# Wider logit tiles in the attention of a hybrid decoder layer: two PSUM banks per tile, one mask-and-maximum instruction for up to 1024 keys

## The chip, the cores and the metric

The kernel runs on one core of one Trainium2 chip. The metric is the device time of one execution in microseconds (us). Engines are named as in the profile: PE is TensorE (PEld its weight loads), DVE is VectorE, ACT is ScalarE, POOL is GpSimd, SP is SyncE.

## The reference: what is computed

One decoder layer on x of 2048 rows by 1024 columns, float32: an RMSNorm, one wide projection, a gated short convolution, a sparse attention, gates, an output projection, a SwiGLU feed-forward part and a last RMSNorm. The change touches the attention alone. There an indexer picks 256 keys for each query, and 8 heads of width 64, which share one set of keys and values, attend to the picked keys with a relative-position bias:

```python
logits = jnp.einsum("bthd,btkd->bhtk", q_b, k_sel) * (HEAD_DIM ** -0.5)
logits = logits + bias[...]
logits = jnp.where(valid[:, None], logits, -jnp.inf)
p = jax.nn.softmax(logits, axis=-1)
o = jnp.einsum("bhtk,btkd->bthd", p, v_sel)
```

The kernel gathers nothing. It takes all causal keys, and an additive mask of large negative numbers removes those that were not picked.

## The kernel before, in words

**Stages.** The kernel first makes all projections (with the index scores between them). Then, for each half of the sequence, it runs the attention of that half (`attention(half)`, L562) and the dense part behind it: branch outputs, output projection, feed-forward. In the first dense part ACT also searches the thresholds for the key masks of the second half.

**Attention of a half.** A half has 8 query blocks of 128 rows, taken from the longest to the shortest (`ORDER`): 7 to 0, then 15 to 8. Block b sees n = (b + 1) * 128 keys. A group is one block with 4 of its 8 heads, so a half has 16 groups. The work of a group has two parts:

- `logits` (L621). For each head the n keys are cut into spans of at most 512 (`cuts`, L610). For each span PE makes the logits with two matmuls (`KH` at L639, `KL` at L640) into the PSUM tile `lg`, which is one bank. One fused DVE instruction (L642) then adds the mask, writes the negated logits into the SBUF tile `pr`, and carries the running maximum `mx` from span to span; its scalar start value is the `mx` of the span before. For all spans but the last the mask is `Mt`, straight from memory. For the last it is `MB`, which POOL prepares: the mask copied to float32 (L617, once for each block and each of two tiles) and, over the last 256 keys, mask plus bias (L629, once for each head). When all spans are done, one ACT instruction (L646) makes the exponentials of the whole row in place.
- `values` (L665). In step sb, for each 128 keys, PE transposes the 4 heads' exponentials into a PSUM tile `tpb` (L686). ACT copies it to `ph` (L689), rounded, and DVE subtracts to get the remainder `pl` (L690). Two matmuls, `ph` (L673) and `pl` (L674), add into the PSUM tile `pv`. `spread` (L653) transposes the reciprocal sums through one more `tpb` tile at the first step of a group (L656, copied out by ACT at L658). At the end of a group ACT copies `pv` to `t` (L678) and POOL scales it.

**PSUM.** Eight banks: `LGB` = 3 for `lg`, `7 - LGB` = 4 for `tpb`, 1 for `pv` (L572 to L574).

**Order of the work.** The order of PE in the attention is written by hand: `in_order` (L590) chains every matmul and transpose behind the one before. Within a step PE issues the logits that are due, the transposes of this step, and the products of three steps earlier (`LAG` = 3). `logits_until` (L723) decides which logits are due: those of a group are spread over the steps of the group before it, span by span, and have to be done `LEAD` steps (5 and 4) ahead of their own group. The queues of ACT, DVE, POOL and SP are ordered by a list scheduler, by priority and by its own forecast of what is ready; once written, each queue is served strictly in order.

**SBUF.** The pools of the attention are stacked from the low end, in the order keys and values, `ap` (with `MB`, `ph`, `pl`, `R`, `t`), `few`, and last the ring of `pr` tiles: 12 of 4 KB per partition in the first half, 9 of 8 KB in the second. The pools of the dense part that follows are stacked from both ends; its `raw4` tiles (4 of 4 KB) and its input tiles `x2`/`y4` (8 of 4 KB) come from the high end. A tile may be filled as soon as the older tiles on its bytes are done with, so the first loads of the dense part can start during the attention: its `raw` tiles take `YT` (the convolution's output) and `AT` (the attention's output). ACT rounds them (`y<-raw`, L130) and DVE takes the remainder (L131), for `AT` after adding two halves (L796). The remainders of the first two are queued on DVE behind the eighth remainder `pl` from the end of the attention (`issue_after`, L809).

Of the kernel before, what the change touches and what calls it, by code (L numbers as in the profile page):

```python
# [25 lines left out]
P = 128  # L26
# [26 lines left out]
SOLO = 4  # L53
LEAD = (5, 4)
PHB = 4
LGB = 3
PRB = (12, 9)
EVERY = 6

# [16 lines left out]
def trunk_kernel(tc, x, g_mix, w_in, b_gate, conv_w, w_a, w_b, w_out, rel_bias,  # L76
# [7 lines left out]
    def pool(stack, name, bufs=1, **kw):  # L84
        return stack.enter_context(tc.tile_pool(name=name, bufs=bufs, reuse_waits="tile", **kw))
# [476 lines left out]
    def attention(half):  # L562
# [6 lines left out]
        few = pool(b_stack, f"few{half}")  # L569
        few.tile([P, 32], F32, name="pad")  # L570
        prp = pool(b_stack, f"pr{half}")
        lgp = pool(b_stack, f"lg{half}", bufs=LGB, space=PSUM)  # L572
        tpb = pool(b_stack, f"tpb{half}", bufs=7 - LGB, space=PSUM)
        pvp = pool(b_stack, f"pv{half}", bufs=1, space=PSUM)  # L574
        biasT = kvp.tile([P, NH, 256], F32, name="biasT")
        KH = kvp.tile([P, LH], F32R, name="KH")
# [20 lines left out]
        def setup(b):  # L597
            n = (b + 1) * P
            c, o = divmod(b * P, CH)
            with tc.high_priority(offset=EARLY):  # L600
                q = kvp.tile([P, NH, P], F32R, name="q", tag="q", bufs=2)
                nc.gpsimd.dma_start(out=q, in_=QS[c][:, :, o:o + P].rearrange("h p t -> p h t"))
                if b < 2:
                    Mt = cadd[:, 2 * P - n:]
                else:
                    Mt = kvp.tile([P, LH], BF16, name="Mt", tag="Mt", bufs=2)
                    nc.gpsimd.dma_start(out=Mt[:, 0:n], in_=MS[b])
                if b == ORDER[half][0]:
                    bias_loads()
            cuts = [0] + list(range(CH - P if n % CH == P and n>P else CH, n, CH)) + [n]  # L610
            spans = [(s0, s1 - s0) for s0, s1 in zip(cuts, cuts[1:])]
            lw = spans[-1][1]
            near = min(lw, 2 * P)
            MBs = [ap.tile([P, CH], F32, name="MB", tag="MB", bufs=4) for _ in range(2)]
            if lw > near:
                for MB in MBs:
                    nc.gpsimd.tensor_tensor(MB[:, 0:lw - near], Mt[:, n - lw:n - near],  # L617
                                            zero.broadcast_to([P, lw - near]), op=ALU.add)
            return b, n, q, Mt, spans, near, MBs

        def logits(st, hg, res):  # L621
# [4 lines left out]
            for hh in range(4):  # L626
# [6 lines left out]
                    pr = prp.tile([P, LH], F32, name="pr", tag="pr", bufs=PRB[half])  # L633
                mx = few.tile([P, 5], F32, name="mx", tag="mx", bufs=6)
                for i, (s0, w) in enumerate(spans):
                    lg = lgp.tile([P, CH], F32, name="lg", tag="lg")
                    for o2 in range(0, w, CH):
                        e2 = min(o2 + CH, w)
                        in_order(nc.tensor.matmul(lg[:, o2:e2], q[:, h, :], KH[:, s0 + o2:s0 + e2], start=True, stop=False))  # L639
# [376 lines left out]
```

## Time and profile before

| | |
|---|---|
| median of 3 runs | 3252.79 us (3252.26 to 3253.07) |
| profiled execution, own time | 3258.31 us |
| its span, first to last instruction | 3256.5 us |
[...]
| attention of the first half | about 980 to 1108 us of the span |
| attention of the second half | about 2037 to 2333 us |

The profiled execution is 5.5 us (0.17%) longer than the median of the timed runs. Durations are taken from it, and differences are applied to the median. A PE that is shown as busy need not be at its peak, since the ends of matmuls are modelled; the start of one matmul to the start of the next is the better measure of what it costs.

### The profile page before, as it was taken

The numbers are of one execution on the slowest core, as the hardware profiler recorded it, in microseconds if no ns is written. First come the engines' busy times: TensorE is split into PE (matmuls) and PEld (weight loads), VectorE is DVE, ScalarE is ACT, GpSimd is POOL, SyncE is SP. The second block draws the span as 40 slices with busy tenths as digits, with TensorE's granted clock in tenths as the row PEclk, the third lists the DMA queues.
The fourth block names the chain that finished last, engine by engine and source line by source line (L and its number), as shares of the span: only waits on it lengthen the run. The fifth ranks groups of instructions, "written<-read, shape, count | busy, mean of one in ns | idle before, by whom it ended". The sixth has DMA issues, their size and how long they took to land.

```text
span 3256.5 us, 41205 instructions
## 1 busy us (share of the span) xinstructions
PE 3183.8 (98%) x14723; PEld 2625.9 (81%) x14723; DVE 1655.4 (51%) x3030; ACT 1877.0 (58%) x3630; POOL 777.5 (24%) x684
## 2 busy tenths in 40 slices
PE   8999999999999899999999999999999999999998
PEld 6788888888887678887888888787788888888887
DVE  6344366663528754654535434898853422332234
ACT  6479888779758685677686780787622211111111
POOL 5411122221115422222221222222122222212221
PEclk9999999999999899999999999999999999999999
DMA  7643233332344861222223223222571411111111
GB/s 233 178 141 118 91 99 95 98 99 88 109 126 110 220 230 51 89 75 87 83 62 95 83 62 101 78 57 73 133 245 47 145 50 46 52 51 46 46 46 52
DMA packets 338630, 324.75 MB, mean 100 GB/s; under 512 B 20340, under 2 KB 268360, under 8 KB 338040
## 3 DMA queue, kind: packets, MB, share of 16 engines
q1 hardware_dynamic: 301800, 293.64, 29.3%
q0 software_dynamic: 36624, 28.48, 4.2%
q8 instruction: 115, 1.88, 0.2%
q14 instruction: 91, 0.75, 0.1%
HBM read 248.09 MB, written 75.54 MB: 99 GB/s over the span
## 4 chain that ended last, share of the span: by engine, by line
PE 73%; ACT 12%; DVE 5%; DMA 5%; issue 3%; POOL 1%; SPq 0%; POOLq 0%; DVEq 0%; ACTq 0%
PE mm L156 8%; PE mm L158 8%; PE mm L157 8%; PE gu L156 7%; PE gu L158 7%; PE gu L157 7%; ACT dump L359 6%; PE dn L156 4%; PE dn L158 4%; PE dn L157 4%; PE tpb L686 3%; PE sc L260 2%; PE sc L259 2%; PE pv L673 2%; PE pv L674 2%
## 5 line engine op out<-in xcount | busy, mean ns | idle before, releaser
L359 ACT ACTIVATE dump<-key,nt 128x384 uint8<-128x384 int16 (+27 forms) x420 | 549.0, 1307 | 10.8
L156 PE MATMUL gu<-h2hi,wgu 128*128 128x512 f32 x1408 | 549.0, 390 | 0.0
L157 PE MATMUL gu<-h2lo,wgu 128*128 128x512 f32 x1408 | 548.5, 390 | 0.0
L158 PE MATMUL gu<-h2hi,wgu 128*128 128x512 f32 x1408 | 548.2, 389 | 0.0
L156 PE MATMUL mm<-hThi,whi 128*128 128x512 f32 (+2 forms) x1216 | 472.3, 389 | 0.2 <-ACT hThi L150 0.2
L158 PE MATMUL mm<-hThi,wlo 128*128 128x512 f32 (+2 forms) x1216 | 470.4, 388 | 0.8 <-POOL wlo L131 0.8
L157 PE MATMUL mm<-hTlo,whi 128*128 128x512 f32 (+2 forms) x1216 | 470.4, 387 | 0.0
L971 DVE SCALAR_TENSOR_TENSOR x<-dn,x 128x512 f32<-128x512 f32 x352 | 240.1, 689 | 221.4 <-PE dn L158 221.2
L267 DVE SCALAR_TENSOR_TENSOR acc<-r,iwT,acc 128x512 f32<-128x512 f32 (+2 forms) x266 | 196.1, 737 | 277.8 <-ACT r L262 276.4
L131 POOL TENSOR_TENSOR wlo<-raw,whi 128x512 fp32r<-128x512 f32 (+1 forms) x132 | 176.1, 1336 | 673.0 <-ACT whi L130 600.2
L131 POOL TENSOR_TENSOR hid<-th,hid 128x512 fp32r<-128x512 f32 x88 | 118.0, 1341 | 823.0 <-ACT hid L130 823.0
L157 PEld LDWEIGHTS gu<-h2lo,wgu 128*128 128x128 f32 x1408 | 264.9, 188 | 55.0
L158 PEld LDWEIGHTS gu<-h2hi,wgu 128*128 128x128 f32 x1408 | 264.8, 188 | 55.1
L156 PEld LDWEIGHTS gu<-h2hi,wgu 128*128 128x128 f32 x1408 | 264.9, 188 | 54.9
L156 PE MATMUL dn<-wd,hid 128*128 128x512 f32 x704 | 275.3, 391 | 5.4 <-ACT hid L130 2.9
L158 PE MATMUL dn<-wd,hid 128*128 128x512 f32 x704 | 274.3, 390 | 1.9 <-POOL hid L131 1.9
L131 POOL TENSOR_TENSOR wgu<-raw,wgu 128x1024 fp32r<-128x1024 f32 x88 | 217.4, 2472 | 242.7 <-ACT wgu L130 236.4
L157 PE MATMUL dn<-wd,hid 128*128 128x512 f32 x704 | 274.6, 390 | 0.0
L158 PEld LDWEIGHTS mm<-hThi,wlo 128*128 128x128 f32 (+1 forms) x1216 | 226.7, 187 | 50.3 <-POOL wlo L131 1.1
L954 DVE SCALAR_TENSOR_TENSOR th<-th,gu 128x512 f32<-128x512 f32 x88 | 60.3, 685 | 403.1 <-ACT th L953 365.7
L157 PEld LDWEIGHTS mm<-hTlo,whi 128*128 128x128 f32 (+1 forms) x1216 | 227.0, 187 | 42.6
L156 PEld LDWEIGHTS mm<-hThi,whi 128*128 128x128 f32 (+1 forms) x1216 | 226.9, 187 | 42.6 <-ACT hThi L150 0.6
(201 smaller groups left out, 5806.2 us busy)
## 6 DMA issues: line engine op xcount, KB each, us to landing
raw<-in_w_in_dram SPq DMA_DIRECT2D x124, 256.0 KB
raw<-in_w_ffn_gate_dram SPq DMA_DIRECT2D x44, 512.0 KB
raw<-in_w_ffn_up_dram SPq DMA_DIRECT2D x44, 512.0 KB
raw<-in_w_ffn_down_dram SPq DMA_DIRECT2D x44, 512.0 KB
S<-SD SPq DMA_DIRECT2D x80, 256.0 KB
GT<-f SPq DMA_DIRECT2D x64, 256.0 KB
ta<-GT SPq DMA_DIRECT2D x64, 256.0 KB
S<-SD SPq DMA_DIRECT2D x68, 192.0 KB
```

The costliest lines, as they stand in the source:

```text
L131: lo_eng.tensor_tensor(lo, raw, hi.bitcast(F32), op=ALU.subtract)
L156: nc.tensor.matmul(ps, whi, xhi, start=start, stop=False)
L157: nc.tensor.matmul(ps, whi, xlo, start=False, stop=False)
L158: nc.tensor.matmul(ps, wlo, xhi, start=False, stop=stop)
L259: nc.tensor.matmul(sc[:, 0:w], iqb[:, h, :], IKH[:, s0:s0 + w], start=True, stop=False)
L260: nc.tensor.matmul(sc[:, 0:w], iqb[:, h, :], IKL[:, s0:s0 + w], start=False, stop=True)
L267: nc.vector.scalar_tensor_tensor(acc[:, 0:w], r[:, 0:w], wv, acc[:, 0:w], op0=ALU.mult, op1=ALU.add)
L359: nc.scalar.activation(dump, keys, AF.Sign, bias=nt, accum_out=sm)
L673: in_order(nc.tensor.matmul(pv, V[:, sb, :], ph, start=sb == 0, stop=False))
L674: in_order(nc.tensor.matmul(pv, V[:, sb, :], pl, start=False, stop=sb == b))
L686: in_order(nc.tensor.transpose(tp[:, hh * P:(hh + 1) * P], Ps[hh][:, sb * P:(sb + 1) * P], ident))
L971: nc.vector.scalar_tensor_tensor(x2[tt][:, ns], ps, 0.5, x2[tt][:, ns], op0=ALU.mult, op1=ALU.add)
```

## The change

The logit tile becomes two banks wide and there are two of them; the transposes keep three banks instead of four. A block with up to 1024 keys has one span, a longer block has two, of which the last holds 768 or 1024 keys. `MB` becomes as wide as the last span can be. The inner loop over `o2`, which is in both versions, cuts the matmuls of a span at 512 columns. Nothing else is edited.

```diff
-LGB = 3
+WIDE = 2 * CH
...
-        lgp = pool(b_stack, f"lg{half}", bufs=LGB, space=PSUM)
-        tpb = pool(b_stack, f"tpb{half}", bufs=7 - LGB, space=PSUM)
+        lgp = pool(b_stack, f"lg{half}", bufs=2, space=PSUM)
+        tpb = pool(b_stack, f"tpb{half}", bufs=3, space=PSUM)
...
-            cuts = [0] + list(range(CH - P if n % CH == P and n>P else CH, n, CH)) + [n]
-            spans = [(s0, s1 - s0) for s0, s1 in zip(cuts, cuts[1:])]
+            first = max(0, n - WIDE)
+            if first and n % CH == P:
+                first += 2 * P
+            spans = [(0, n)] if first == 0 else [(0, first), (first, n - first)]
             lw = spans[-1][1]
             near = min(lw, 2 * P)
-            MBs = [ap.tile([P, CH], F32, name="MB", tag="MB", bufs=4) for _ in range(2)]
+            MBs = [ap.tile([P, WIDE], F32, name="MB", tag="MB", bufs=4) for _ in range(2)]
...
-                    lg = lgp.tile([P, CH], F32, name="lg", tag="lg")
+                    lg = lgp.tile([P, WIDE], F32, name="lg", tag="lg")
                     for o2 in range(0, w, CH):
                         e2 = min(o2 + CH, w)
```

## Rows read from the trace of the kernel before

**Rows 1.** The profile page, busy time of PE and its weight loads, and of the other engines: share of the span and number of instructions.

```profile
PE 3183.8 (98%) x14723; PEld 2625.9 (81%) x14723; DVE 1655.4 (51%) x3030; ACT 1877.0 (58%) x3630; POOL 777.5 (24%) x684
```

**Rows 2.** Busy time of each engine by stretch. Columns: stretch and its length in us, then busy us (and instructions) of PE, PEld, DVE, ACT, POOL, then the granted clock, the DMA share and GB/s. The first row is 84 us of the first half's attention, the second the whole attention of the second half, the others 40 us pieces of that.

```profile
978.00:1062.00 84.00, 80.30 (x464) 65.19 (x463) 73.49 (x202) 69.24 (x145) 44.94 (x64) 1.00 0.44 106
2037.00:2336.00 299.00, 285.36 (x1664) 234.61 (x1663) 272.65 (x673) 229.26 (x366) 73.13 (x95) 0.99 0.25 72
...
2080.00:2120.00 40.00, 39.94 (x238) 33.68 (x237) 37.31 (x94) 31.63 (x47) 7.75 (x10) 1.00 0.18 49
2200.00:2240.00 40.00, 37.11 (x215) 30.25 (x214) 35.01 (x84) 29.80 (x50) 10.80 (x14) 1.00 0.36 93
```

**Rows 3.** Timeline of one steady step in the second half, PE and DVE. Columns: start us, duration us, engine, line, operation, tiles, size, count merged into the row.

```profile
2120.10 0.60 PE L686 MATMUL tpb<-ident,pr 128*128 128x128 f32 x4
...
2120.45 0.47 PE L673 MATMUL pv<-ph,V 128*128 128x512 f32 x1
...
2120.76 0.39 PE L674 MATMUL pv<-pl,V 128*128 128x512 f32 x1
...
2120.99 0.39 PE L639 MATMUL lg<-KH,q 128*128 128x512 f32 x1
...
2121.22 0.40 PE L640 MATMUL lg<-KL,q 128*128 128x512 f32 x1
...
2121.45 0.60 PE L686 MATMUL tpb<-ident,pr 128*128 128x128 f32 x4
2121.65 0.75 DVE L642 CUSTOM_DVE_ANT_0 pr<-lg,Mt,mx 128x512 f32<-128x512 f32 x1
...
2122.33 0.09 DVE L642 DVE_READ_ACCUMULATOR2_ANT mx<- 128x1 f32 x1
```

**Rows 4.** Groups of instructions by shape, second half (2037 to 2334). Columns: count, busy us, mean ns of one, idle us before them and what ended it.

```profile
L690 DVE TENSOR_TENSOR pl<-tpb,ph 128x512 fp32r<-128x512 f32 x200 | 132.5, 684 | 6.4 <-ACT ph L689 6.0
...
L642 DVE CUSTOM_DVE_ANT_0 pr<-lg,Mt,mx 128x512 f32<-128x512 f32 x96 | 71.7, 747 | 11.2 <-PE lg L640 7.1 <-PE tpb L686 0.5
...
L642 DVE CUSTOM_DVE_ANT_0 pr<-lg,MB,mx 128x256 f32<-128x256 f32 x32 | 15.3, 477 | 0.5 <-DVE mx L642 0.3
```

**Rows 5.** Timeline around one exponential in the second half: ACT, PE and DVE.

```profile
2124.05 1.80 ACT L646 ACTIVATE pr<-pr,mx 128x1792 f32<-128x1792 f32 x1 [0.22 <-DVE mx L642]
...
2124.27 0.60 PE L686 MATMUL tpb<-ident,pr 128*128 128x128 f32 x4
...
2125.84 1.09 ACT L689 ACTIVATE ph<-tpb 128x512 fp32r<-128x512 f32 x2
...
2127.87 1.28 DVE L690 TENSOR_TENSOR pl<-tpb,ph 128x512 fp32r<-128x512 f32 x2
...
2128.13 0.60 PE L686 MATMUL tpb<-ident,pr 128*128 128x128 f32 x4
...
2128.81 0.39 PE L674 MATMUL pv<-pl,V 128*128 128x512 f32 x1
```

**Rows 6.** Timeline, single turns of the `tpb` tiles: two rows of the first half, then two from the start and two from the end of the second half's attention.

```profile
992.93 0.60 PE L686 MATMUL tpb<-ident,pr 128*128 128x128 f32 x4
...
993.47 0.69 DVE L690 TENSOR_TENSOR pl<-tpb,ph 128x512 fp32r<-128x512 f32 x1
...
2058.06 0.60 PE L686 MATMUL tpb<-ident,pr 128*128 128x128 f32 x4
2058.31 0.24 ACT L658 COPY row<-tpb 4x128 f32<-4x128 f32 x1
...
2328.65 0.60 PE L686 MATMUL tpb<-ident,pr 128*128 128x128 f32 x4
...
2330.00 2.48 DVE L690 TENSOR_TENSOR pl<-tpb,ph 128x512 fp32r<-128x512 f32 x4
```

**Rows 7.** Timeline, the two matmuls of a 128-column span in block 0.

```profile
1088.54 0.27 PE L639 MATMUL lg<-KH,q 128*128 128x128 f32 x1
1088.65 0.27 PE L640 MATMUL lg<-KL,q 128*128 128x128 f32 x1
```

**Rows 8.** Groups by shape, first half: POOL's copy of the mask.

```profile
L617 POOL TENSOR_TENSOR MB<-Mt,zero 128x256 f32<-128x256 bf16 x4 | 2.4, 610 | 5.5 <-DMA Mt<-MS 5.5
...
L617 POOL TENSOR_TENSOR MB<-Mt,zero 128x128 f32<-128x128 bf16 x4 | 1.5, 401 | 0.0
```

**Rows 9.** Timeline, the start of both attentions on ACT and DVE: the rounding of the first `YT` piece, the end of the fourth head's maximum, and the fourth head's exponential, first half and second half.

```profile
984.87 1.06 ACT L130 ACTIVATE y<-raw 128x1024 fp32r<-128x1024 f32 x1 [3.46 <-DMA raw<-YT]
...
987.06 0.08 DVE L642 DVE_READ_ACCUMULATOR2_ANT mx<- 128x1 f32 x1
...
989.23 1.14 ACT L646 ACTIVATE pr<-pr,mx 128x1024 f32<-128x1024 f32 x1
...
2046.41 1.06 ACT L130 ACTIVATE y<-raw 128x1024 fp32r<-128x1024 f32 x1 [30.81 <-DMA raw<-YT]
...
2051.03 0.09 DVE L642 DVE_READ_ACCUMULATOR2_ANT mx<- 128x1 f32 x1
...
2053.33 1.99 ACT L646 ACTIVATE pr<-pr,mx 128x2048 f32<-128x2048 f32 x1
```

**Rows 10.** Timeline, PE waiting for a logit tile behind a DVE that had waited for an `AT` load, one row of each half.

```profile
1077.70 0.50 PE L639 MATMUL lg<-KH,q 128*128 128x256 f32 x1 [3.26 <-DVE mx L642]
...
2212.86 0.50 PE L639 MATMUL lg<-KH,q 128*128 128x512 f32 x1 [1.63 <-DVE mx L642]
```

## The prediction

> **What bounds the kernel now.** I read the page first: PE is busy nearly all the time and DVE half of it [rows 1]. A share over the whole kernel hides its stages, so I then read busy time by stretch. In the dense stages DVE is far from full; in the attention it is not. In the steady part of the second half PE is busy 39.94 of 40 us and DVE 37.31 [rows 2], so two engines are close to their limit at once, and the question is which of them sets the step.
>
> The timeline of one step answers it [rows 3]. From the first transpose of one step (2120.10) to that of the next (2121.45) PE needs 1.35 us: 0.35 for four transposes, 0.31 and 0.23 for the two products, twice 0.23 for the logits of 512 keys. PE goes from each to the next without a gap. DVE has one logit instruction (2121.65 to 2122.33, 0.68) and one remainder of 0.68 [rows 3, 4], together 1.36. So both are at their limit, but it is DVE that is seen to wait for PE's logits, 7.1 us in all [rows 4], and what PE does is no less after the change: 200 steps of 0.89 and 400 matmuls of 0.23 are 270 of the 296 us of the second half's attention. I take PE as what paces it, and DVE as a queue with almost no reserve.
>
> **What becomes of a transposed tile.** This is the thing to see, as the change takes a bank from it. In the step of 2124.27 the transposes are followed by an exponential of 1.80 us on ACT, which began at 2124.05, so `ph` starts at 2125.84, and `pl` is the first of two that DVE makes from 2127.87, ended at 2128.55 [rows 5]. PE's product with this `pl` starts at 2128.81, and the transposes three steps on start at 2128.13 [rows 5]. So in steps with an exponential the remainder comes some 0.3 us before its product and 0.4 us after the third transposes that follow. With four tiles that is in time; with three it isn't.
>
> **The change, part by part.**
>
> *DVE instructions.* A head has 1, 1, 1, 1, 2, 2, 2, 2 spans in blocks 0 to 7 and 3 (four times) and 4 (four times) in blocks 8 to 15. After the change it is one and two. With 8 heads 32 instructions go in the first half and 96 in the second. A 512-key instruction lasts 747 ns, a 256-key one 477 [rows 4]: 1.055 ns a key and 207 ns fixed, of which 70 lie under the next instruction (0.75 long, next start after 0.68 [rows 3]). So 0.14 us are saved for each, 4 and 13 us; one for 1024 keys takes 0.75 + 0.54 - 0.07 = 1.22 us from start to start, where two took 1.36. On the path this is nothing as long as PE paces. What it can give is a shorter queue before each `pl`. Bounds 0 and -4 (a quarter of the 17, about the share of steps with an exponential); I take -2.
>
> *Transposed tiles, four to three.* I went through the `tpb` tiles in order and asked, with all times as they are, whether the tile three turns back was read out when the next one started. In the second half 28 of 216 turns would be late, by 10.8 us in sum and 2.03 at most: the first at 2058.06, where the copy of the reciprocals ends at 2058.55, the last at 2328.65, where the remainder three turns back ends at 2330.68 [rows 6]. They gather at the start of groups, where the reciprocals take a turn of their own. In the first half up to 1080 it is 11 turns, 4.1 us in sum, and the worst is 1.23 at 992.93 (remainder ended at 994.16 [rows 6]). PE's delay is a lasting loss, but it lets DVE catch up, so neighbouring late turns count once: the bounds are the worst alone (2.0 and 1.2) and the sum (10.8 and 4.1). I take the middle, 6.0 and 2.4.
>
> *Larger steps.* Logits now come as four matmuls (0.92 us) every second step instead of two in each. Between transposes and their product lie then 3.6 or 4.5 us in turn, not 4.05, and a `pl` that queues behind a logit instruction waits up to 1.22 instead of 0.68. Products of the second half that were ready by less than that 0.54 would be late by 3.7 us in sum, and with 0.45 more taken off by 9.2; only half of the steps get shorter. Bounds 0 and 9.2 (3.0 in the first half); I take 3.0. For the logit tiles themselves the slack grows: a tile is needed again after two of 2.7 us, not three of 1.35.
>
> *Block 4.* Its 640 keys were 384 and 256 and become 512 and 128 columns in one span. A 128-column matmul costs 0.11 [rows 7], 512 cost 0.23 [rows 3]; 384 and 256 lie in proportion at 0.17 and 0.12. That is +0.05 for 16 matmuls, +0.8. In all other blocks the pieces keep their widths and change places. Blocks 0 to 3 have one span before and after.
>
> *POOL.* The mask copies grow from at most 256 to at most 768 columns: 1.63 ns a column and 0.19 fixed [rows 8], so 1.44 us each, two for a block, some 8 us more in the first half and 18 in the second on an engine that is busy 45 of 84 and 73 of 299 us [rows 2]. Queued behind them is the bias add of the block's first head, and its DVE instruction waits for that; the lead of four or five steps, 5 us or more, covers the 3.6. Cost 0; without that cover up to 3.6 at a block's start.
>
> *SBUF.* `MB` adds 8 KB, so the `pr` ring moves up by 8 KB, and its topmost buffer then covers the first `raw` tile of the dense part. The first `YT` piece can no longer be loaded at the start of the attention, and must wait for that buffer's last user, a head of the last block but one that uses the ring (block 3, block 9). Its remainder is queued behind the end of the attention anyway. Cost 0 while that holds. In the second half the second head's `pr` then also lies on the `x2` tiles stored last, so its first DVE instruction waits for that store; behind it DVE's queue waits, but the fourth exponential starts 2.2 us after the maximum it needs [rows 9], so that is covered too.
>
> *Sum:* 6.0 + 2.4 + 3.0 + 0.8 - 2.0 = +10.2 us. The profiled execution (3258.3, span 3256.5) lies 5.5 over the median; on the median the forecast is 3263.
>
> **The rivals.**
>
> *Nothing measurable.* The shorter DVE queue gives as much as the three tiles take: DVE's share falls by 13 in 273 us [rows 2], and the late turns are late by 0.4 us on average. The lower ends add up to 2.0 + 1.2 + 0 + 0.8 - 4 = 0, so 3253. Against it stands the step of rows 5, which has no reserve.
>
> *Faster, since DVE was the pacemaker.* Its 1.36 is as long as PE's 1.35 [rows 3]. If DVE is what PE really follows, the 17 us come off, less the 2 to 4 that late turns cost at the least: 3240. It decides if DVE's idle before L642 [rows 4] is only where PE had been held by DVE earlier. Against it: PE shows no gap in the step. [...]
>
> *Faster, since loads leave the heads of the queues.* At both starts ACT waits for the first `YT` piece before the exponentials; the fourth exponential starts 2.1 and 2.2 us after its maximum [rows 9]. Twice DVE holds PE behind an `AT` load, 3.3 and 1.6 us [rows 10]. If the move in SBUF takes the loads off these places and nothing else comes in, that is -9 to -11: 3243. Against it: the second `YT` piece still finds a free tile and may stand in the same place.
>
> *Slower still, by a late dense part.* If the first `YT` piece of the second half is loaded only at the end of the attention, its load, rounding and remainder stand before the first branch matmul: some 7 us on top, 3270.
>
> **How the numbers follow.** A measurement of this kernel can tell about 0.2%, 6.5 us, from no change. Forecast 0.45, late dense part 0.07: slower 0.52. Nothing measurable 0.30. DVE pacemaker 0.08, queue heads 0.10: faster 0.18. The forecast's own range is 3255 to 3280 (lower ends, and the upper ends 10.8 + 4.1 + 9.2 + 3.0 + 0.8 = 28). To leave out no more than 2 in 10 the range goes down to 3245, short of the two faster cases' centres.
>
> **What would show it.** Right: DVE busy lower by 13 to 17 us over both attentions, the 1024-key instruction near 1.29 us long; waits of PE's transposes for `pl` (L686 behind L690) of several us in sum, standing at the starts of groups; both attentions longer, the dense parts not. Wrong: steps under 1.35 us on PE's side (then DVE paced it), or transposes that don't wait (then the reserve was there), or a difference that stands outside the attentions.

## The result and the profile after

The changed kernel takes 3284.14 us (median of 4 runs, 3283.19 to 3285.13) against 3252.53 for the kernel before: slower, ratio 1.0098 with a 95% interval of 1.0085 to 1.011, or 28 to 36 us. The prediction was 3263, range 3245 to 3280. The direction was right and the size was not: 31.6 us on the medians, where 10.2 were forecast.

Below, a **difference** is the ratio's difference from 1, times 3253. A **stretch** is read from one profile. It runs from the start of one instruction to the start of another, and a branch matmul is here one that takes `y` (L156 to L158). Five stretches are used throughout: *start 1* (last projection matmul to the first transposes), *half 1* (from there to the last branch matmul), *start 2* (last matmul of the first dense part to the first transposes), *half 2* (to its last branch matmul), and *dense 1* (last branch matmul of the first half to that part's last matmul), whose code is the same in all kernels. Dense 1 took from 856.8 to 862.9 us over all profiles, so a stretch is known to some 3 us. And the profile of before lies 5.5 us above its median while that of after lies 0.5 above: the stretches of before are up to 5.5 long in sum, and differences from them are small by as much.

| us | before | after | difference |
|---|---|---|---|
| start 1 | 9.7 | 14.8 | +5.1 |
| half 1 | 184.4 | 187.4 | +3.0 |
| start 2 | 15.5 | 18.5 | +3.0 |
| half 2, up to the last product with `V` | 280.1 | 285.8 | +5.7 |
| half 2, rest of the branch stage | 67.7 | 80.1 | +12.4 |

Dense 1 and all that follows half 2 differ by -2.0 and -0.5. Nearly half of the loss stands in the branch stage behind the second attention, and 8.1 us at the two starts. These are places for which the prediction had a cost of nothing. Where a loss stands in a profile is not yet what causes it: with the causes of these three taken away, the time will stand elsewhere (e10 below).

The page of after, busy time and instructions, as [rows 1]:

```profile
PE 3193.8 (97%) x14723; PEld 2631.2 (80%) x14723; DVE 1645.2 (50%) x2774; ACT 1881.3 (57%) x3630; POOL 804.4 (25%) x696
```

Busy time by stretch, columns as in [rows 2]; the first row is the first half, the second the second attention, the third a steady piece of it:

```profile
978.00:1062.00 84.00, 74.97 (x422) 61.16 (x422) 63.20 (x124) 63.82 (x129) 46.86 (x63) 0.96 0.37 83
2044.00:2347.00 303.00, 284.75 (x1656) 233.98 (x1656) 252.91 (x472) 224.81 (x359) 87.99 (x103) 0.98 0.20 53
2090.00:2130.00 40.00, 38.57 (x231) 32.44 (x229) 34.16 (x58) 30.47 (x46) 10.84 (x14) 1.00 0.18 50
```

DVE got its relief: 252.91 us busy in the second attention, 19.7 less than before. About 8.5 of these are work of the dense parts (9 instructions of L131, L796 and L971 in the window of before, none in that of after), so some 11 are the wide instruction's. PE, 39.94 of 40 before, now has 1.4 us of gaps in 40.

Groups by shape in the second attention (2044 to 2347), columns as in [rows 4]:

```profile
L692 DVE TENSOR_TENSOR pl<-tpb,ph 128x512 fp32r<-128x512 f32 x200 | 132.2, 686 | 26.3 <-ACT ph L691 25.5
L688 PE MATMUL tpb<-ident,pr 128*128 128x128 f32 x800 | 120.7, 273 | 7.0 <-DVE pl L692 5.2 <-ACT row L660 1.5
...
L644 DVE CUSTOM_DVE_ANT_0 pr<-lg,MB,mx 128x1024 f32<-128x1024 f32 x48 | 61.4, 1279 | 7.4 <-PE lg L642 6.1 <-DVE mx L644 0.3
...
L619 POOL TENSOR_TENSOR MB<-Mt,zero 128x768 f32<-128x768 bf16 x10 | 14.5, 1462 | 17.5 <-DMA Mt<-MS 17.5
```

The 1024-key instruction is 1279 ns long (1290 forecast), the 768-column copy 1462 ns (1440 from [rows 8]). DVE now waits 25.5 us for ACT's `ph`, before 6.0: it is further from its limit than it was (34.16 of 40 us in the steady piece, 37.31 before). The transposes wait for `pl` and for the copy of the reciprocals, as forecast.

**A late turn.** Timeline of after, PE, DVE and ACT around one group start; in brackets the idle time before and what ended it:

```profile
2125.47 1.28 DVE L644 CUSTOM_DVE_ANT_0 pr<-lg,MB,mx 128x1024 f32<-128x1024 f32 x1 [0.63 <-PE lg L642]
...
2126.68 1.88 DVE L692 TENSOR_TENSOR pl<-tpb,ph 128x512 fp32r<-128x512 f32 x3
...
2127.52 0.63 PE L688 MATMUL tpb<-ident,pr 128*128 128x128 f32 x4 [1.18 <-DVE pl L692]
...
2130.27 0.24 ACT L660 COPY row<-tpb 4x128 f32<-4x128 f32 x1
...
2130.57 0.65 PE L688 MATMUL tpb<-ident,pr 128*128 128x128 f32 x4 [0.25 <-ACT row L660]
```

Three remainders have queued up behind one logit instruction of 1.28 us. The first frees its tile at about 2127.4, and the transposes that need it start at 2127.52, after 1.18 us without work. Two steps later they wait again, for the copy that empties the reciprocals' tile: the next transposes take that very tile. In the built program the tiles aren't handed out in a fixed ring, but as the scheduler expects them to come free: in six of the sixteen groups of the second attention the transposes behind the reciprocals have the same bank as these (sequences such as 4, 5, 5, 6), in the kernel before in none. In [rows 5] the same kind of moment had a fourth tile to go on with.

**Start 1.** POOL and DVE of after at the start of the first attention:

```profile
979.11 1.32 POOL L631 TENSOR_TENSOR MB<-Mt,biasT 128x256 f32<-128x256 bf16 x2 [0.39 <-DMA biasT<-BS]
983.63 2.46 POOL L619 TENSOR_TENSOR MB<-Mt,zero 128x640 f32<-128x640 bf16 x2 [3.20 <-DMA Mt<-MS]
986.05 2.56 POOL L631 TENSOR_TENSOR MB<-Mt,biasT 128x256 f32<-128x256 bf16 x4
```

```profile
982.47 1.22 DVE L644 CUSTOM_DVE_ANT_0 pr<-lg,MB 128x1024 f32<-128x1024 f32 x1
...
988.02 1.23 DVE L644 CUSTOM_DVE_ANT_0 pr<-lg,MB 128x1024 f32<-128x1024 f32 x1 [4.32 <-POOL MB L631]
```

By the order and the sizes of these rows the list scheduler has put the mask copies of block 6 (640 columns) and two bias adds ahead of the third bias add of block 7. POOL waits 3.20 us for block 6's mask, copies for 2.46, and makes the two adds. Only the third of the four adds is, by its end at about 988.0, the one that block 7's third head needs; DVE, idle for 4.32 us, goes on at 988.02. PE then starts again, at 989.31 and at a granted clock of 0.50 (989 to 993), where the kernel before has 1.00 over this whole start [rows 2]; ahead of that it had stood idle for 4.36 us. The window, with the columns of [rows 2]:

```profile
989.00:993.00 4.00, 3.69 (x9) 2.67 (x10) 2.72 (x7) 2.59 (x5) 1.51 (x3) 0.50 0.00 0
```

**Start 2 and the branch stage.** Timeline of after, the second half: DVE at the start; then SP, DVE and ACT behind the attention:

```profile
2049.38 1.22 DVE L644 CUSTOM_DVE_ANT_0 pr<-lg,Mt 128x1024 f32<-128x1024 f32 x1 [3.04 <-DMA X<-x]
...
2342.50 0.98 SPq L791 DMA_DIRECT2D raw<-YT  x2
2344.63 2.69 SPq L797 DMA_DIRECT2D raw<-AT  x4
...
2355.05 1.22 DVE L798 TENSOR_TENSOR raw<-raw,raw 128x1024 f32<-128x1024 f32 x1 [2.22 <-DMA raw<-AT]
...
2356.31 1.06 ACT L130 ACTIVATE y<-raw 128x1024 fp32r<-128x1024 f32 x1 [5.08 <-DVE raw L798]
```

The `pr` ring now lies on the first `raw` tile. So not one `YT` piece but both, and the `AT` pieces behind them, are loaded only when the ring is done with, at 2342 us and after; before, ACT rounded the first piece at 2046.41 [rows 9]. What was spread over the attention now stands in a row: load, add of the halves, rounding, remainder. The two waits of [rows 10] are gone from the attentions with it. The first matmuls of the branch stage, by what they waited for, in before (2334 to 2401) and after (2348 to 2428):

```profile
L156 PE MATMUL gu<-y,wab 128*128 128x512 f32 x64 | 26.2, 409 | 4.1 <-ACT wab L130 4.0
```

```profile
L156 PE MATMUL gu<-y,wab 128*128 128x512 f32 x64 | 27.5, 433 | 10.2 <-ACT y L130 5.1 <-ACT wab L130 5.1
```

### The profile page after: what moved, and what is told of

Same layout as the page of the kernel before. It is cut to its first block, busy times and chain, and to the rows that moved or that the text cites. A ratio compares the mean times of both kernels' runs of the same rounds, so it can differ in the third digit from the quotient of the medians.

```text
span 3282.8 us, 40959 instructions
## 1 busy us (share of the span) xinstructions
PE 3193.8 (97%) x14723; PEld 2631.2 (80%) x14723; DVE 1645.2 (50%) x2774; ACT 1881.3 (57%) x3630; POOL 804.4 (25%) x696
## 4 chain that ended last, share of the span: by engine, by line
PE 72%; ACT 11%; DVE 6%; DMA 5%; issue 4%; POOL 1%; SPq 0%; POOLq 0%; DVEq 0%; ACTq 0%
PE mm L156 8%; PE mm L158 8%; PE mm L157 8%; PE gu L158 7%; PE gu L156 7%; PE gu L157 7%; ACT dump L359 6%; PE dn L158 5%; PE dn L156 5%; PE dn L157 5%; PE tpb L688 3%; PE sc L260 2%; PE sc L259 2%; PE pv L675 2%; PE lg L641 2%
## 5 line engine op out<-in xcount | busy, mean ns | idle before, releaser
L359 ACT ACTIVATE dump<-key,nt 128x384 uint8<-128x384 int16 (+27 forms) x420 | 549.0, 1307 | 10.8
L156 PE MATMUL gu<-h2hi,wgu 128*128 128x512 f32 x1408 | 548.6, 390 | 0.0
L158 PE MATMUL gu<-h2hi,wgu 128*128 128x512 f32 x1408 | 548.2, 389 | 0.0
L156 PE MATMUL mm<-hThi,whi 128*128 128x512 f32 (+2 forms) x1216 | 472.7, 389 | 0.0
L158 PE MATMUL mm<-hThi,wlo 128*128 128x512 f32 (+2 forms) x1216 | 470.5, 388 | 0.5 <-POOL wlo L131 0.5
L131 POOL TENSOR_TENSOR wlo<-raw,whi 128x512 fp32r<-128x512 f32 (+1 forms) x132 | 175.6, 1331 | 674.7 <-ACT whi L130 618.3
L131 POOL TENSOR_TENSOR hid<-th,hid 128x512 fp32r<-128x512 f32 x88 | 119.1, 1354 | 819.9 <-ACT hid L130 819.9
L156 PEld LDWEIGHTS gu<-h2hi,wgu 128*128 128x128 f32 x1408 | 264.7, 188 | 54.9
L158 PEld LDWEIGHTS gu<-h2hi,wgu 128*128 128x128 f32 x1408 | 264.6, 188 | 54.8
L156 PE MATMUL dn<-wd,hid 128*128 128x512 f32 x704 | 275.3, 391 | 4.6 <-ACT hid L130 2.3
L131 POOL TENSOR_TENSOR wgu<-raw,wgu 128x1024 fp32r<-128x1024 f32 x88 | 218.0, 2479 | 244.1 <-ACT wgu L130 238.6
L158 PE MATMUL dn<-wd,hid 128*128 128x512 f32 x704 | 274.7, 391 | 1.9 <-POOL hid L131 1.9
L158 PEld LDWEIGHTS mm<-hThi,wlo 128*128 128x128 f32 (+1 forms) x1216 | 226.7, 187 | 50.0 <-POOL wlo L131 0.7
L156 PEld LDWEIGHTS mm<-hThi,whi 128*128 128x128 f32 (+1 forms) x1216 | 226.9, 187 | 42.3 <-ACT hThi L150 0.4
```

Of the source, the lines that this page charges most:

```text
L131: lo_eng.tensor_tensor(lo, raw, hi.bitcast(F32), op=ALU.subtract)
L156: nc.tensor.matmul(ps, whi, xhi, start=start, stop=False)
L158: nc.tensor.matmul(ps, wlo, xhi, start=False, stop=stop)
L359: nc.scalar.activation(dump, keys, AF.Sign, bias=nt, accum_out=sm)
```

## Experiments

Four theories: **the moved ring** (late loads, the store wait), **the copies** in POOL's queue, **the tiles** (three for transposes instead of four), **the portions** (up to 1024 columns of logits between two transposes). The prediction had the last two as its whole cost, and nothing for the first two. All differences are against the kernel before.

### One part of the change at a time

**e1_room**, the ring moved and nothing else:

```diff
+        ap.tile([P, 4 * CH], F32, name="room")
```

> The kernel before with an unused 8 KB tile per partition beside the mask tiles: the ring of probability rows and all above it sit where the changed kernel has them, nothing else differs. Theory A (the moved ring holds back the first loads of the branch stage and the mask copies of the second half): 3262 to 3267 us, with the first YT piece of the second half loaded after 2330 us instead of at 2042 us and the branch stage after it about 10 us longer; in the first half the early rounding of YT, which stood in ScalarE's queue there, is gone, which may give back 2 to 4 us. The prediction, which costed the move at nothing: 3252 to 3254 us.

Measured: 3264.71, +11 us (8 to 15). The `YT` and `AT` loads of the second half stand at the end of the attention, as in after:

```profile
2321.87 0.99 SPq L790 DMA_DIRECT2D raw<-YT  x2
2323.99 2.73 SPq L796 DMA_DIRECT2D raw<-AT  x4
```

Start 2 is 3.6 us longer. The second attention up to its last product is 7.0 shorter (273.1) and the stage behind it 10.2 longer (78.0): early loads cost something while they are early, and more when they are late. The theory stands.

**e2_three_tiles**, three tiles for the transposes, and four one-bank logit tiles, which is as many banks as the change gives them:

```diff
-LGB = 3
+LGB = 4
```

> The kernel before with four one-bank logit tiles and three transposed tiles instead of three and four; operations and their sizes are those of before. The prediction (transposes wait 2.4 us in the first half and 6.0 us in the second for the subtraction that frees their tile): 3258 to 3262 us, with new waits of tpb on VectorE's pl. Rival theory A, by which nearly all of the 32 us comes from what the larger mask tile displaces: 3252 to 3255 us.

Measured: 3266.18, +13 us (9 to 17), above both expectations. Half 1 is 5.1 longer, half 2 6.0. In the second attention the transposes now wait 3.8 us for `pl`, before not at all. In half 1 several waits change at once: those for `pl` grow from 3.7 to 7.8 us, those for `t` shrink from 8.1 to 3.7, and one stands ahead of a matmul of the branch stage, where the kernel before has none over 1.5 us:

```profile
1138.26 0.76 PE L156 MATMUL gu<-o,wab 128*128 128x512 f32 x1 [5.32 <-ACT o L130]
```

So it is open how much of half 1's loss is that of the transposed tiles.

**e3_pool_copies**, as many copied columns as in after, in pieces of up to 256:

```diff
+                more = wide - (lw - near)
+                while more > 0:
+                    w = min(more, near)
+                    nc.gpsimd.tensor_tensor(MB[:, lw - near:lw - near + w], ...)
+                    more -= w
```

> The kernel before with GpSimd copying as many mask columns per block as the changed kernel does (the extra ones in pieces of up to 256 columns into the same 512-wide mask tiles), nothing else changed. Theory B (the copies stand in GpSimd's queue ahead of bias adds and make VectorE late at a block's start): 3255 to 3258 us, most of it ahead of the first transposes of each half. The prediction, which costed them at nothing: 3252 to 3254 us.

Measured: 3258.58, +6 us (3 to 9). Start 2 is 3.7 us longer and start 1 0.7; the rest isn't to be found in the stretches (half 2 is 1.9 shorter than in the profile of before). That POOL's copies cost nothing is refuted.

**e4_steps**, the portions alone, on narrow tiles:

```diff
-                    if i < len(spans) - 1:
+                    if i == len(spans) - 3:
                         yield
...
-                    yield g, (i + 1) / (4 * len(blocks[b][4]))
+                    yield g, (i + 1) / (4 * min(2, (len(blocks[b][4]) + 1) // 2))
```

> The kernel before with its narrow tiles and operations, but its logits issued in the changed kernel's portions: up to 1024 columns at a time between two transposed blocks, not 512. The prediction (3.0 us for larger steps): 3255 to 3257 us. If a larger portion makes the product wait for its probabilities at every step: 3260 us or more. If three narrow logit tiles absorb it: 3252 to 3254 us.

Measured: 3257.80, +5 us (3 to 8). No stretch of its profile shows it (half 1 +0.5, half 2 -2.5).

The four add up to 36 us, the change to 32. That these are close proves nothing: in the runs below, the ring and the copies together cost less within the change than apart.

### The side effects taken out of the changed kernel

**e5_ring_back**, the mask tiles above the ring instead of below it:

```diff
+        mbp = pool(b_stack, f"mb{half}")
         lgp = pool(b_stack, f"lg{half}", bufs=2, space=PSUM)
...
-            MBs = [ap.tile([P, WIDE], F32, name="MB", tag="MB", bufs=4) for _ in range(2)]
+            MBs = [mbp.tile([P, WIDE], F32, name="MB", tag="MB", bufs=4) for _ in range(2)]
```

> The changed kernel with its mask tiles in a pool above the ring of probability rows, so that the ring and its neighbours no longer move up by 8 KB. Theory A (the moved ring costs what the unused 8 KB did): 3270 to 3274 us, the first YT piece of the second half loaded at about 2045 us again and the branch stage after it about 66 us from its first product to its last, not 76. If the larger operations, not the ring, make that stage late: 3282 to 3286 us. The mask tiles of the second half now lie where the last x2 tiles are stored from, so the mask copies may still wait for those stores.

Measured: 3286.47, +33 us (29 to 38): nothing gained. `YT` was loaded at 2337.67, because now the mask tiles lay on the first `raw` tile. The experiment didn't remove what it was to remove, so it is no test of the theory by its time. Its profile does show something: its branch stage behind the second attention is short again (66.4 us) and its second attention long (293.9): the loads still come ahead of the attention's last steps, and there it loses its time (to the 180th of 200 key steps both kernels take 266.4 us, for the rest 27 and, in after, 19). Half 2 as a whole is 360.3, 5.7 below after; half 1 is 3.2 and start 2 1.5 longer.

**e6_copies_behind**:

```diff
+                    if len(adds) == 8:
+                        stack.enter_context(tc.issue_after(adds[-3].ins))
                     for MB in MBs:
                         nc.gpsimd.tensor_tensor(MB[:, 0:lw - near], ...)
```

> The changed kernel with the mask copies of each half's second block queued on GpSimd behind the seventh of the first block's eight bias additions, not behind the second. Theory B (the copies, waiting for their mask, hold up the bias additions that the first block's second head group needs): the first transposes of the first half come 4 to 5 us earlier (at about 990 us, not 994.65) and the time is 3278 to 3281 us. If something else is late there: 3282 to 3286 us.

Measured: 3277.19, +24 us (20 to 29), 7 below after. The first transposes start at 989.92, and start 1 takes 9.6 us, as in the kernel before.

**e7_ring_and_copies**, both edits:

> Both of these edits of the changed kernel at once. If the two side effects add up: 3265 to 3270 us, what stays being the third transposed tile (13 us in the experiment that had it alone) and the wider operations. If the two overlap: 3270 to 3276 us.

Measured: 3279.86, +26 us (22 to 30); like e5, with the ring's place still covered (`YT` at 2334.59).

**e9_masks_elsewhere**, e5 with the pool at the far end:

```diff
+        mbp = pool(b_stack, f"mb{half}", side="right")
```

> The changed kernel with its mask tiles on the other side of the memory, above everything that the branch stage loads early, so that the probability ring now ends 8 KB below where it ended before. Placing them above the ring brought nothing, since there the mask tiles themselves covered the place of the first loads; here nothing does. Theory A (late loads cost 11 us, as with the unused 8 KB): 3270 to 3275 us, YT of the second half loaded at about 2045 us, the branch stage after it 66 us long. If the late loads only change the order of work that is late anyway: 3280 to 3286 us.

Measured: 3278.91, +26 us (21 to 30), 5 below after. The loads are early again,

```profile
2048.40 0.88 SPq L792 DMA_DIRECT2D raw<-YT  x2
```

the stage behind the second attention takes 67.8 us, not 80.1, but the attention itself takes 292.5, not 285.8: the early loads bring 12.4 there and take 6.7 here. In half 1, by the profiles, they only take: 192.2, not 187.4. Theory A has the mechanism right and overstates the net.

**e10_masks_and_copies**, e9 with e6:

> The same with the mask copies of each half's second block behind the seventh bias addition, which alone brought 7 us. If the two side effects are separate: 3264 to 3269 us, 11 to 16 us above the kernel before, of which the third transposed tile has 13 us by its own experiment. If wide operations cost something of their own beside that: 3270 us or more.

Measured: 3276.72, +23 us (20 to 28), 7 below after. Both starts are at their old length (9.0 and 14.7). POOL and DVE at the first start, to be held beside those of after:

```profile
978.98 1.32 POOL L635 TENSOR_TENSOR MB<-Mt,biasT 128x256 f32<-128x256 bf16 x2 [0.47 <-DMA biasT<-BS]
982.93 0.68 POOL L635 TENSOR_TENSOR MB<-Mt,biasT 128x256 f32<-128x256 bf16 x1 [2.64 <-DVE mx L648]
984.08 0.67 POOL L635 TENSOR_TENSOR MB<-Mt,biasT 128x256 f32<-128x256 bf16 x1 [0.47 <-DVE mx L648]
...
984.25 1.23 DVE L648 CUSTOM_DVE_ANT_0 pr<-lg,MB 128x1024 f32<-128x1024 f32 x1 [0.25 <-PE lg L646]
```

The third head's add runs at 982.93 and its DVE instruction at 984.25, 3.8 us earlier. With both side effects undone, 23 us remain, far more than the 11 that the prediction gave for tiles and portions. They stand in half 1 (195.0, 10.5 longer) and in the second attention (293.0, 12.9 longer).

Two things follow. On top of e6, which left the ring where it was, undoing the ring is worth 1 us (24 to 23), which can't be told from nothing: by the profiles it brings 6.9 us in start 2 and half 2 and costs 10.2 in half 1. And the loss of half 1 is hardly one of transposed tiles: PE waits 1.5 us there for `pl` and the copy of the reciprocals, and 3.7 before. Its largest wait stands behind the last attention steps, ahead of a matmul of the branch stage:

```profile
1152.06 0.76 PE L156 MATMUL gu<-o,wab 128*128 128x512 f32 x1 [9.56 <-ACT dump L359]
```

What holds it wasn't tested. In e6 and in after, with the late loads, no wait of half 1 is longer than 3.7 us.

### What remains: tiles, portions, or the wide instruction

**e11_tiles_and_steps**, e2 and e4 together, with narrow instructions only:

> The kernel before with four narrow logit tiles, three transposed tiles and the changed kernel's portions of up to 1024 columns: the same tile budget and the same order of issue as the change, with operations of 512 columns. From the single experiments (13.2 and 5.2 us): 3266 to 3272 us if they add; 3262 to 3266 us if the larger portions cost nothing once a fourth logit tile is there.

Measured: 3275.50, +21 us (17 to 25). Half 1 is 9.9 longer, half 2 11.5. This has e10's tile budget for the transposes and e10's order of issue, but none of its wide instructions, and its time is e10's, 2 us apart. DVE is 260.35 us busy in its second attention and 247.40 in e10's: the 13 us that were forecast, and no time came of them. At this order of issue the wide instruction shows neither a cost nor a gain. The two kernels also differ in the mask copies and in SBUF, so that a gain and a cost that cancel aren't excluded.

**e12_fine_portions**, e10 with a yield between the two 512-column parts of a tile:

> The kernel of the second run here with its logits issued in portions of 512 columns again: a wide tile is filled by two portions with transposes between them, and the fused operation follows the second. If the portion's size costs the 3 to 5 us that the prediction and its own experiment gave it: 3 to 5 us below that run. If what costs is that a two-bank tile is only freed by one long operation: equal to it or slower by up to 5 us, since the tile is held longer.

Measured: 3276.17, +23 us (19 to 27), the same as e10. So small portions give nothing back here. Held beside e2, which has small portions and three transposed tiles as well but narrow instructions, it is slower: 23 against 13 us, half 2 11.4 longer instead of 6.0. With narrow tiles the large portions cost some 8 us on top of the three tiles, with wide tiles nothing: the wide tile, or what comes with it (mask copies, places in SBUF), costs about as much in their stead. The waits for `t` fall from 7.7 to 4.1 us in the second attention, and the transposes of the reciprocals wait 2.7 us for a tile in place of 0.7.

**e15_three_and_three**, e11 with three logit tiles and a bank left empty:

> The kernel before with three narrow logit tiles, three transposed tiles and an empty bank, issued in portions of up to 1024 columns. With four logit tiles the same came to 3275.5 us. If the missing transposed tile is the cause of that: 3272 to 3279 us again. If the fourth logit tile took part (logits running further ahead of the transposes): 3262 to 3268 us.

Measured: 3270.23, +18 us (14 to 22), between the two. Half 2 is 13.7 longer, so there three transposed tiles with large portions are enough for the loss, and the fourth logit tile has no part in it. Half 1 is only 1.8 longer, where e11 had 9.9.

**e16_row_tile_apart**, three transposed tiles, small portions, and the reciprocals in a tile of their own:

```diff
+        rcp = pool(b_stack, f"rc{half}", bufs=1, space=PSUM)
...
-            tp = tpb.tile([P, CH], F32, name="tpb", tag="tpb")
+            tp = rcp.tile([P, CH], F32, name="rc", tag="rc")
```

> The kernel before with three transposed tiles and the transposed reciprocals, which take a turn of the same ring once per head group, in a tile of their own. If the turn of the reciprocals (held until ScalarE has copied the row) is what makes three tiles too few: 3252 to 3256 us. If three are too few at every step, for the subtraction on VectorE: 3260 to 3268 us, as with three shared tiles.

Measured: 3263.11, +10 us (6 to 14). Half 2 is 1.4 longer, where e2 had 6.0; half 1 4.4, where e2 had 5.1. The reciprocals' turn is a good part of the loss in the second half, not the loss.

**e13_five_tiles** (`LGB = 2`) and **e14_two_products** (`LGB = 2`, four transposed tiles, `bufs=2` for `pv`):

> The kernel before with two narrow logit tiles and five transposed tiles: the other step along the line on which four and three cost 13 us. If each transposed tile below some need costs, and four are enough: 3252 to 3256 us, or above if two logit tiles make VectorE wait. If four were already short: 3243 to 3250 us.

> The kernel before with two narrow logit tiles, four transposed tiles and two tiles for the products with the values, which in the kernel before wait for the copy of the one tile (4.4 us in the second half, 8.1 us in the first). If a second one frees these waits and two logit tiles suffice: 3242 to 3249 us. If the third logit tile was needed: 3256 us or more.

Measured: 3267.21, +13 us (8 to 17), and 3256.65, +3 us (0 to 6). A fifth transposed tile doesn't make up for the logit tile that it takes, and the third logit tile is needed at the starts: with two, start 1 takes 14.3 and 14.2 us, start 2 18.0 and 17.7. Two tiles for the products do take the waits for `t` away (in the second attention 4.4 us in before, none in e14).

What PE waited for in the second attention (first transposes to last product with `V`), columns: the waiting instruction, the releaser, us in total, times, longest. In order: before, e11, e10, e14.

```profile
PE pv L673 <- ACT t L678: 4.4, 6, 1.2
PE tpb L686 <- ACT pr L646: 2.3, 2, 1.7
PE lg L639 <- DVE mx L642: 1.6, 1, 1.6
...
```

```profile
PE pv L673 <- ACT t L678: 8.0, 12, 1.5
PE tpb L686 <- DVE pl L690: 5.4, 7, 2.1
PE tpb L686 <- ACT pr L646: 1.7, 1, 1.7
PE tpb L686 <- ACT row L658: 0.8, 2, 0.5
...
```

```profile
PE tpb L692 <- DVE pl L696: 9.7, 10, 1.8
PE pv L679 <- ACT t L684: 7.7, 10, 1.7
PE tpb L692 <- ACT row L664: 1.5, 3, 1.0
...
```

```profile
PE lg L639 <- DVE mx L642: 3.9, 6, 2.4
PE pv L674 <- DVE pl L690: 1.9, 4, 0.7
...
```

In the second attention no transposes wait for `pl` with four tiles or more; with three, they do in every run, for 4 us (e2, e16) to 10 (e10) in sum. In the first half they wait for it with four tiles too, 3.7 us in before. The larger portions show in another place: the wait for `t`, the copy that frees the product tile at the end of a group, goes from 4.4 to 8 us (6.4 in e4).

### Is there a version that beats both?

**e8_late_rounding**, the kernel before with its early roundings queued later:

```diff
-        with tc.issue_after(ends[-MG].ins):
+        k = len(ends) // 4
+        with tc.issue_after(ends[k].ins), tc.issue_after(acts[k].ins):
```

> The kernel before with the rounding of the first two YT pieces queued on ScalarE and VectorE behind a quarter of the half's transposed blocks, and that of the first AT pieces behind three quarters, the loads left early. The experiment with the unused 8 KB ran both attention halves faster (by 12 us and by 5 us from first to last transposes) while its branch stage came late. If that was the early roundings leaving the queue heads: 3240 to 3249 us. If it came from elsewhere: 3252 to 3256 us.

Measured: 3255.00, +1 us (-2 to 4). The roundings leave the starts and nothing is gained, so their place in the queues wasn't what made the second attention of e1 shorter. There the work had left the attention altogether.

**e17_ramp_in_turn**, e14 with every second logit tile of the first group taken from the transposed tiles, and **e18_ramp_and_rounding**, the same with e8:

> The kernel before with two narrow logit tiles, four transposed and two product tiles, and every second logit tile of a half's first head group taken from the transposed tiles, which are idle then. With two product tiles both attention halves were shorter (by 2.6 and 4.8 us) while the first logits, on two tiles, came to their first transposes 4.5 and 2.3 us later. If tiles were what was missing there: 3244 to 3249 us. If the start is late for another reason (a queue): 3251 to 3257 us.

> The same with the early roundings of the branch stage queued later, as in the experiment on them, which alone moved 2 us within the second half and nothing that its runs could tell. If the two add up: 3242 to 3247 us; if not: as the run beside it.

Measured: 3255.60, +2 us (-1 to 5), and 3256.24, +3 us (0 to 6). Start 2 is back at 15.6, start 1 only at 12.2 and 11.1, and the 4.8 us that e14 had won in half 2 have shrunk to 0.6. No version was found that beats the kernel before.

## Why the prediction was right in direction and wrong in size

- **PE paces the attention: right.** DVE was 19.7 us less busy in the second attention and the time rose. On the same tile budget and order of issue, wide (e10) and narrow (e11) instructions take the same time though DVE is 13 us less busy with the wide ones. The rival by which DVE was the pacemaker is refuted. The fixed part per instruction that the prediction read from [rows 3, 4], 0.14 us from start to start, was saved: the 1024-key instruction has the forecast length, 1279 ns. It was saved off the path. The credit of 2 us for a shorter queue isn't seen in any run.
- **Tiles, four to three: right in kind, too small.** The forecast was 6.0 and 2.4. Alone (e2) it costs 13 us (9 to 17) by the runs. By the profile the second half has the 6.0, and the first 5.1, not 2.4. In the second half the mechanism is the one described: remainders behind a logit instruction, the reciprocals' turn, waits at group starts; that the 6.0 came out to the digit is luck, since it was picked between 2.0 and 10.8. What failed is the first half, which was read only up to 1080 us, and there as "the middle" between the worst turn and the sum. Behind that, where the attention meets the branch stage, stand waits that the forecast doesn't have (5.32 us in e2, 9.56 in e10). The count of late turns also looked three turns back each time; the turn after the reciprocals can get their tile, one turn back, and waits for ACT's copy (1.5 us in the second attention of after, none before).
- **Portions: mis-sized as a term of their own.** The forecast was 3.0, to be added. Alone (e4) they cost 5 us (3 to 8). With the tiles (e11) the two cost 21 us (17 to 25), where 11.4 were forecast, and half 2 is 5.5 us longer than with the tiles alone, while the portions alone do not lengthen it. The step that failed is the price of these two together; by the runs it is little over what they cost apart (18.5), by the profile of half 2 well over it (11.5 against 6.0 and nothing). They may use the same reserve: a step whose product waited for `t` comes late to its transposes, and now there is no fourth tile to catch up with. That is argued from the waits above, not shown; e12, whose portions are small and whose waits for `t` are down to 4.1 us, is as slow, so portions aren't the only way to this loss.
- **SBUF: a cost of nothing that failed.** Cost 0 was given because the first piece's remainder is queued behind the attention anyway. This looked at one piece. The loads behind it on SP and in the `raw` tiles were late with it, and ACT and DVE did then in a row what had been done beside the attention. Alone (e1) this costs 11 us (8 to 15). Undone within the changed kernel it is 5 (e9), and 1 once the copies are out of the way (e10 against e6): the attentions that the early loads lie in are longer by the profiles (e9 against after: 6.7 us in the second, 4.8 in half 1). The wait for the stored `x2` was foreseen with its place, and its cover, the late fourth exponential, was not there: DVE waited 3.04 us at 2049.38. The rival "late dense part" named this mechanism and gave it 7 us and a chance of 0.07; it came beside the forecast, not in its place.
- **POOL: the other zero that wasn't.** The bound was 3.6 us at a block's start "without that cover", the cover being a lead of four or five steps. At the start of a half there is no lead, for the first group's logits are what everybody waits for. And the order in POOL's queue was taken to be that of the program; the list scheduler put block 6's copies, which wait for a load, ahead of block 7's third add. Undone (e6): 7 us. The copies alone (e3): 6 us (3 to 9).
- **Queue heads and nothing measurable: refuted.** The early roundings left the queue heads, at the starts with e8 and in after, and no time came of it on balance: in e1 the second attention is 7.0 us shorter, and what follows 10.2 longer. And 28 to 36 us are clear of the 6.5 that the prediction took for what a measurement can tell from nothing.
- **The sum.** Two things in it failed. The tiles and the portions were put at 11.4 us, term by term, and with them the kernel takes 21 (e11) to 23 us (e10) more. The moved ring and POOL's copies were put at nothing, and together they are the other 7 to 9 of the 32. The forecast's upper ends (28 us) held the first, and had nothing for the second. One of the prediction's own signs of being wrong came true with it: a difference that stands outside the attentions, in the branch stage and at the starts.

**Open.** The first half, which has 10 of the 21 to 23 us: e10 has 10.5 us more there, e11 9.9, and e15, with one logit tile less than e11, 1.8; e6, wide but with late loads, 0.4. The order in which the scheduler mixes the first branch matmuls with the last steps of the attention differs (in e11 the first is at 1098.67, in e15 at 1109.41 us), and in e11 PE waits 9.7 us, put down to DVE's `ta`, behind them, but no experiment held that order fixed. So it isn't shown how much of this half's loss is the tile budget's and how much that order's. Open too is where e4's 5 us lie, and why wide tiles with small portions (e12) cost more than narrow ones (e2).

## What to carry to other kernels

A cost of nothing is worth its cover's proof at the worst place, not in the steady state: the start of the first attention had no lead, and there POOL's queue, served strictly in order, passed on the wait of the instruction at its head: 3.20 us for block 6's mask, and behind it DVE idle for 4.32 us and PE for 4.36 (7 us of the time, by e6). When a tile grows in one memory, list what its neighbours now lie on, and follow every load that needs those bytes and all that is queued behind it, not the first one alone. And losses in one kernel needn't add: here the two side effects cost 17 us apart and 7 to 9 together, and in the second half tiles and portions cost 11.5 together, 6.0 and nothing apart. Try them together, or give the sum a wider range than that of its terms.

## What the hardware showed that was not expected

A fused instruction that takes its start value from an SBUF column (`mx`) was longer than one with a constant: 1279 ns against 1224 for 1024 columns, 1012 against 952 for 768, all with the mask from `MB`. No run shows why. And the pause at the first start of after (4.36 us without a matmul) was followed by a granted clock of 0.50 (989 to 993), with twelve 512-column matmuls up to the first transposes, most at 0.43 us from start to start, where most of those ahead of the pause have 0.23. That is 2.4 us, an estimate from these numbers. That the pause brought the low clock is the author's reading of one place: e10, without the pause, has 1.00 from 981 to 993, and no run changed the pause alone. If it did, it cost its own length as idle time and about half as much again as slow matmuls.
